# Later modulation sections summed by GpSimd during attention, inverse sums broadcast by DMA

## The chip, the core and the metric

The kernel runs on one core of one Trainium2 chip. The metric is device time in microseconds (us). The kernel before was run three times: 2298.46 us median, 2298.4 lowest, 2302.22 highest. Durations below come from one further execution under the profiler.

## The reference, cut to what matters

The reference is one layer of a block with two branches, in float32, for 1024 latent and 256 context tokens of width 1024. A conditioning vector `c` gives six modulation sections of 1024 numbers each (numbered here 0 to 5, in the order of the last line):

```python
silu_c = jax.nn.silu(c)
mod = (silu_c @ w_mod[l] + b_mod[l])[:, None, :]
sh1, sc1, g1, sh2, sc2, g2 = jnp.split(mod, 6, axis=-1)
h = rmsnorm(x, norm1_g[l]) * (1.0 + sc1) + sh1
y, yc = token_mix(h, hc, ...)
x = x + g1 * y
x = x + g2 * swiglu(rmsnorm(x, norm2_g[l]) * (1.0 + sc2) + sh2, ...)
```

`token_mix` projects `h`, runs an mLSTM scan in two directions and a grouped-query attention (8 query heads, 2 key/value heads, 1280 keys), and merges both through `w_pa`, `w_pb` and `w_o`. Sections 0 and 1 are wanted at the very start; sections 2 (`g1`), 3 (`sh2`), 4 (`sc2`) and 5 (`g2`) only behind attention.

## The kernel before

Float32 products are made of three fp32r matmuls (`mm3`, lines 104 to 106): each operand is split into a high part (ScalarE, line 98) and a low part (line 99, on GpSimd or VectorE). A planner in `run` hands out projection units one after another; a tile framework then orders every engine's queue, each queue runs in order, and semaphores do the rest. Loads and stores go through SP's queue for the most part.

The stages in time: the projections (to about 780 us) and the mLSTM heads (to about 1000 us), merging that branch with `w_pa`, attention (about 1072 to 1392 us), the `w_pb` stage (to about 1545 us), the `w_o` stage, and the feed-forward part.

**Modulation.** `mod_block` (line 285) loads 512 columns of `w_mod` in four DMAs of 512 KB and multiplies them on TensorE with `sc`, the silu of `c`, in eight float32 matmuls (line 300, tile `macc`); VectorE copies the result out (line 304). `modulation_rest` (line 333) does one half of a later section with it. For sections 2 and 5 one more matmul (line 344, tile `mg`) gives a row, VectorE adds the bias, and a DMA writes the row to `d_g`; for sections 3 and 4 four matmuls with one column (line 312, tile `mch`) turn it to channels for `B2` and `A2`. It is called eight times: after projection units 14 and 15 (line 1281, section 2), after column blocks n = 1, 2, 4 and 5 of the `w_pb` loop (line 1396, sections 3 and 4), and once in each half of the `w_o` loop (line 1508, section 5).

**Attention** (line 1083) goes through 64 steps: 2 key/value groups, 8 tiles of 128 tokens, 4 heads. A step makes scores for the next head (tile `sc`, maxima by line 1033), transposes the probabilities of this one (line 1054, tile `pt`, evacuated by lines 1057 and 1058 into `PT`), and does a part of the value products of the tile before (`attn_values`, tile `av`, `part` = the head). PSUM banks with tag Y, two of them, serve all transposes. The inverse row sums go into columns 0, 32, 64 and 96 of a 128x128 tile `dg`, which GpSimd zeroes for every tile (line 1100). In part 1 `dg` is transposed (line 1071), copied to `rrow` (line 1073), and GpSimd broadcasts four rows of it over the partitions into `rs` (line 1076). In part 3 VectorE multiplies `av` by `rs` into `yaf` (line 1080). `attn_group_kv` (line 992) splits v with the low part on GpSimd; `attn_q` (line 1012) loads the queries of a tile into the single buffer `qr`.

Of the kernel before, what the change touches and what calls it, by code (L numbers as in the profile page):

```python
# [9 lines left out]
F32 = mybir.dt.float32  # L10
F32R = mybir.dt.float32r
AF = mybir.ActivationFunctionType
ALU = mybir.AluOpType
# [4 lines left out]
P = 128  # L18
D = 1024
KT = D // P  # L20
S = 1024
CT = 256
NT = S // P
# [64 lines left out]
class Block:  # L88
# [241 lines left out]
                    nc.vector.tensor_tensor(t, v, bm[:, 8 + k:10 + k], op=ALU.add)  # L330
                    nc.vector.scalar_tensor_tensor(out=self.A1[:, s, k:k + 2], in0=t, scalar=1.0, in1=g1[:, k:k + 2], op0=ALU.add, op1=ALU.mult)

    def modulation_rest(self, ps, i):

        nc = self.nc
        bm = self.ch("b_mod")
        j0, b = (2, 5, 3, 4)[i // 2], i % 2
        c0 = j0 * D + b * 512
        rows = self.mod_block(ps, "X", (c0, c0 + 256))
        if i < 4:  # L340
            row = self.slots.get([P, 1024], F32)
            nc.sync.dma_start(row[0:1, 0:512], self.io["b_mod"][0:1, c0:c0 + 512])
            o = ps("Y", "mg")
            nc.tensor.matmul(o[0:2, :], lhsT=self.sel, rhs=rows[:, 0], start=True, stop=True)
            nc.vector.tensor_tensor(row[0:1, 512:1024], o[0:1, :], row[0:1, 0:512], op=ALU.add)
            nc.sync.dma_start(self.d_g[i // 2:i // 2 + 1, b * 512:(b + 1) * 512], row[0:1, 512:1024])
            self.slots.put(rows, row)
            return
        m = self.mod_channels(rows, ps, "Y", 1)[:, :, 0]
        hs = slice(4 * b, 4 * b + 4)  # L350
        if j0 == 3:
            nc.vector.tensor_tensor(self.B2[:, hs], m, bm[:, 24 + 4 * b:28 + 4 * b], op=ALU.add)
        else:
            t = self.st.tile([P, 4], F32, name="modt2", tag="modt2", bufs=2)
            nc.vector.tensor_tensor(t, m, bm[:, 32 + 4 * b:36 + 4 * b], op=ALU.add)
            nc.vector.scalar_tensor_tensor(out=self.A2[:, hs], in0=t, scalar=1.0, in1=self.ch("norm2_g")[:, hs], op0=ALU.add, op1=ALU.mult)


    def first_loads(self):
# [632 lines left out]
    def attn_group_kv(self, pool, ps, g):  # L992
        nc = self.nc
        kt = [pool.tile([P, NP * P], F32R, name="kT%d" % i, tag="kT%d" % i, bufs=2) for i in range(2)]
        vv = [pool.tile([P, NP, AD], F32R, name="vv%d" % i, tag="vv%d" % i, bufs=1) for i in range(2)]
        for q in range(5):
            kr = pool.tile([P, 2, AD], F32, name="kr", tag="kr", bufs=2)
            nc.sync.dma_start(kr, self.d_k[q * 256:(q + 1) * 256, g * AD:(g + 1) * AD].rearrange("(t p) d -> p t d", p=P))
            vr = pool.tile([P, 2, AD], F32, name="vr", tag="vr", bufs=2)
            nc.sync.dma_start(vr, self.d_v[q * 256:(q + 1) * 256, g * AD:(g + 1) * AD].rearrange("(t p) d -> p t d", p=P))  # L1000
            tp = ps("Y", "pt")
            for i in range(2):
                nc.tensor.transpose(tp[:, i * P:(i + 1) * P], kr[:, i], self.idf)
            sl = slice(q * 256, (q + 1) * 256)
            nc.scalar.activation(kt[0][:, sl], tp[:, 0:256], AF.Copy)
            nc.vector.tensor_tensor(kt[1][:, sl], tp[:, 0:256], kt[0][:, sl].bitcast(F32), op=ALU.subtract)
            self.split(vv[0][:, 2 * q:2 * q + 2], vv[1][:, 2 * q:2 * q + 2], vr)
        return kt, vv

    SEGS = ((0, 512), (512, 512), (1024, 256))  # L1010
# [49 lines left out]
    def attn_values(self, pool, ps, g, t, PT, vv, dg, ya, part):  # L1060

        nc = self.nc
        if part == 0:
            self.av = ps("Z", "av")
        av = self.av
        for s in ((0, 1, 2), (3, 4), (5, 6, 7), (8, 9))[part]:
            pt = PT[s // 4]
            self.mm3(av, (vv[0][:, s], vv[1][:, s]), (pt[0][:, s % 4], pt[1][:, s % 4]), s == 0, s == NP - 1)
        if part == 1:
            rb = ps("Y", "pt")  # L1070
            nc.tensor.transpose(rb[:, 0:P], dg, self.idf)
            rows = pool.tile([P, P], F32, name="rrow", tag="rrow", bufs=1)
            nc.vector.tensor_copy(rows, rb[:, 0:P])
            self.rs = pool.tile([P, 512], F32, name="rs", tag="rs", bufs=1)
            for h in range(4):
                nc.gpsimd.partition_broadcast(self.rs[:, h * P:(h + 1) * P], rows[32 * h:32 * h + 1, :])
        if part < 3:
            return
        rs = self.rs
        nc.vector.tensor_tensor(ya[:, 4 * g:4 * g + 4, t * P:(t + 1) * P], av.rearrange("p (h t) -> p h t", h=4),  # L1080
                                rs.rearrange("p (h t) -> p h t", h=4), op=ALU.mult)

    def attention(self, pool, ps):


        nc = self.nc
        kv, qs, dgs = {}, {}, {}
        kv[0] = self.attn_group_kv(pool, ps, 0)
        qs[0, 0] = self.attn_q(pool, ps, 0, 0)
        steps = [(g, t, h) for g in range(2) for t in range(NT) for h in range(4)]  # L1090

        def scores(i):
            if i >= len(steps):
                return None
            g, t, h = steps[i]
            if h == 0:
                if (g, t) not in qs:
                    qs[g, t] = self.attn_q(pool, ps, g, t)
                dgs[g, t] = pool.tile([P, P], F32, name="dg", tag="dg", bufs=2)
                nc.gpsimd.memset(dgs[g, t], 0.0)  # L1100
            sc, st = self.attn_scores(pool, ps, h, qs[g, t], kv[g][0])
            return lambda: self.attn_exp(pool, h, sc, st, dgs[g, t])

# [3 lines left out]

        yield
        pr = scores(0)()
        ptp, ya = yield  # L1110
        PT, pend = None, None
        for i, (g, t, h) in enumerate(steps):
            if g == 0 and t == NT - 2 and h == 0:
# [11 lines left out]
            if h == 3:  # L1125
                pend = (pool, ps, g, t, PT, kv[g][1], dgs[g, t], ya)
            pr = nxt() if nxt else None
        for part in range(4):
            self.attn_values(*pend, part)
        yield  # L1130
# [2 lines left out]
    def run(self):  # L1133
        nc, tc, io = self.nc, self.tc, self.io
# [8 lines left out]
        def scratch(name, shape):  # L1143
            return dr.tile(shape, F32, name=name)
# [12 lines left out]
        self.d_mm = scratch("d_mm", [D, S])  # L1157
        self.d_ms = scratch("d_ms", [D, S])
        self.d_x1 = scratch("d_x1", [S, D])
        self.d_act = scratch("d_act", [FT // 2, 7, P, 512])  # L1160

        self.const, close_const = pool("const")
# [22 lines left out]
        slots = self.slots = Slots()  # L1185
# [64 lines left out]
        X, later = {}, []  # L1250
# [5 lines left out]
        for i, u in enumerate(units):  # L1256
# [20 lines left out]
                more()  # L1277
            if i == 13:
                slots.put(*[t for p in self.cT for t in p])
            if i in (14, 15):  # L1280
                self.modulation_rest(PS, i - 14)
            if i == 22:
                while later:
                    more()
# [63 lines left out]

        pt, close_pt = pool("pt")
        w_pb = [self.load_s(slots, io["w_pb"], 0, KT, n * P, P) for n in range(2)]  # L1350
        attn.send((pt, yaf))
        close_pt()
        close_pa()

# [21 lines left out]
        for n in range(KT):  # L1376
# [15 lines left out]
                self.split(hi[:, n % 2], lo[:, n % 2], t[:, 0])  # L1392
                slots.put(t)
            slots.put(*w)
            if n in (1, 2, 4, 5):
                self.modulation_rest(PS, 3 + n if n < 3 else 2 + n)
            if n >= KT - 2:
                load_o(0, (0, 1) if n == KT - 2 else (2, 3))
        for half in range(2):
# [85 lines left out]
        for half in range(2):  # L1485
# [7 lines left out]
            for b in range(2):  # L1493
                c = slice(b * 512, (b + 1) * 512)
                for t in range(4):
# [8 lines left out]
                    if b:  # L1504
                        r0 = (4 * half + t) * P
                        nc.sync.dma_start(self.d_x1[r0:r0 + P, :], x1[t])
                if not b:
                    self.modulation_rest(PS, 2 + half)
                if half:
                    for j in range(4):  # L1510
                        slots.put(*w_o[b, j])
# [204 lines left out]
        acc = {}  # L1716
# [128 lines left out]
```

## Time and profile before

| | |
|---|---|
| median of 3 runs | 2298.46 us |
| profiled execution, whole time | 2302.7 us |
| its span, first to last instruction | 2300.6 us |
| mean granted TensorE clock | 0.979 |
| TensorE matmul busy | 2164.7 us (94%) |
| VectorE, ScalarE, GpSimd busy | 1566.8, 983.6, 755.6 us |
| DMA | 258.18 MB, mean 112 GB/s |

Whole time and span differ by 2.1 us, which lie around the first and last instruction. Times in rows count from the span's start. A matmul's duration runs longer than the distance to the next one, because matmuls are pipelined; the distance between starts is what a matmul costs.

### The profile page before, as it was taken

The page shows a single profiled execution, that of the slowest core. Times are in us where ns is not written, and L with a number is a line of the kernel's source. Part 1 is how long each engine was busy: PE and PEld are TensorE (multiplying, and loading weights), DVE is VectorE, ACT ScalarE, POOL GpSimd, SP SyncE. Part 2 cuts the span into 40 slices and gives each one's busy share as a digit, 9 for nine tenths or more (in the row PEclk, how much of TensorE's full clock was granted, in tenths as well). Part 3 has the DMA queues.
Part 4 walks back from the last instruction along what each step waited for, and adds up shares of the span by engine and source line. Part 5 has one row for each costly group of instructions (what it writes and reads, how often), then busy time and mean ns, then how long its engine had stood idle before and what let it go on. Part 6 is the DMA issues. An engine that isn't in the chain of part 4 may idle for free. (4 is left out here: it accounts for less than half of the span.)

```text
span 2300.6 us, 30283 instructions
## 1 busy us (share of the span) xinstructions
PE 2164.7 (94%) x11003; PEld 1779.5 (77%) x11003; DVE 1566.8 (68%) x2827; ACT 983.6 (43%) x1957; POOL 755.6 (33%) x615
## 2 busy tenths in 40 slices
PE   5899999999999698999999998999899999998996
PEld 2698888977978587877888886777688888876875
DVE  4767566476788777676887883345846454578997
ACT  4434435243443464543777763124523232334333
POOL 1422222321323231211101004321554544457765
PEclk9999999999999899999999999999899999999998
DMA  7122323244232813128000005652143333364421
GB/s 261 55 84 90 112 92 105 83 127 139 78 119 74 304 59 116 43 86 279 16 17 23 17 16 183 205 213 76 46 133 96 110 96 110 105 230 165 163 83 74
DMA packets 173301, 258.18 MB, mean 112 GB/s; under 512 B 13008, under 2 KB 111320, under 8 KB 173152
## 3 DMA queue, kind: packets, MB, share of 16 engines
q1 hardware_dynamic: 163232, 232.43, 30.6%
q10 hardware_dynamic: 9920, 23.82, 2.7%
q8 instruction: 87, 1.43, 0.2%
q14 instruction: 62, 0.51, 0.1%
HBM read 185.91 MB, written 70.30 MB: 111 GB/s over the span
## 5 line engine op out<-in xcount | busy, mean ns | idle before, releaser
L98 ACT ACTIVATE s<-s 128x1024 fp32r<-128x1024 f32 (+2 forms) x438 | 360.6, 846 | 661.2 <-DVE s L233 68.7
L104 PE MATMUL pr<-s,s 128*128 128x512 f32 (+1 forms) x1736 | 624.1, 361 | 19.3 <-DVE s L261 10.0
L106 PE MATMUL pr<-s,s 128*128 128x512 f32 (+1 forms) x1736 | 622.4, 359 | 7.8 <-POOL s L99 4.7
L105 PE MATMUL pr<-s,s 128*128 128x512 f32 (+1 forms) x1736 | 623.0, 359 | 5.8 <-POOL s L99 4.1
L99 POOL TENSOR_TENSOR s<-s,s 128x1024 fp32r<-128x1024 f32 (+1 forms) x195 | 397.3, 2048 | 659.8 <-ACT s L98 517.9
L99 DVE TENSOR_TENSOR s<-s,s 128x1024 fp32r<-128x1024 f32 (+2 forms) x243 | 303.8, 1258 | 131.7 <-ACT s L98 108.3
L104 PEld LDWEIGHTS pr<-s,s 128*128 128x128 f32 x1736 | 331.6, 191 | 75.6 <-ACT s L98 12.5
L106 PEld LDWEIGHTS pr<-s,s 128*128 128x128 f32 x1736 | 331.0, 191 | 60.4 <-POOL s L99 6.8
L105 PEld LDWEIGHTS pr<-s,s 128*128 128x128 f32 x1736 | 331.4, 191 | 56.7 <-POOL s L99 5.3
L104 PE MATMUL pj<-s,s 128*128 128x512 f32 x568 | 227.9, 402 | 19.3 <-DVE s L1743 14.5
L105 PE MATMUL pj<-s,s 128*128 128x512 f32 x568 | 225.6, 397 | 7.3 <-POOL s L99 7.3
L106 PE MATMUL pj<-s,s 128*128 128x512 f32 x568 | 224.7, 396 | 0.7 <-POOL s L99 0.7
L261 DVE TENSOR_TENSOR s<-s,pr 128x512 f32<-128x512 f32 x200 | 133.3, 681 | 87.8 <-PE pr L106 83.2
L1533 DVE TENSOR_TENSOR s<-s,pr 128x512 f32<-128x512 f32 x154 | 100.0, 679 | 112.3 <-ACT s L1549 63.1
L104 PEld LDWEIGHTS pj<-s,s 128*128 128x128 f32 x568 | 108.7, 191 | 54.7 <-DVE s L1743 18.5
L1058 DVE TENSOR_TENSOR PT<-pt,PT 128x512 fp32r<-128x512 f32 (+1 forms) x192 | 112.5, 598 | 33.2 <-ACT PT L1057 31.1
L1043 ACT ACTIVATE pr<-sc,st 128x512 f32<-128x512 f32 (+1 forms) x192 | 118.2, 623 | 34.4 <-DVE st L1035 34.1
L105 PEld LDWEIGHTS pj<-s,s 128*128 128x128 f32 x568 | 108.8, 192 | 30.2 <-POOL s L99 7.7
L106 PEld LDWEIGHTS pj<-s,s 128*128 128x128 f32 x568 | 108.8, 192 | 24.3 <-POOL s L99 1.1
L1543 POOL TENSOR_TENSOR s<-s,s 128x512 f32<-128x512 f32 x44 | 70.0, 1593 | 165.2 <-ACT s L98 87.6
L1057 ACT ACTIVATE PT<-pt 128x512 fp32r<-128x512 f32 (+1 forms) x192 | 94.6, 525 | 54.4 <-PE pt L1054 54.1
L1033 DVE TENSOR_REDUCE st<-sc 128x1 f32<-128x512 f32 (+1 forms) x192 | 109.6, 591 | 0.8 <-PE sc L106 0.8
(313 smaller groups left out, 3503.8 us busy)
## 6 DMA issues: line engine op xcount, KB each, us to landing
s<-in_w_in_dram SPq DMA_DIRECT2D x60, 512.0 KB
d_act<-s SPq DMA_DIRECT2D x74, 256.0 KB
s<-d_act SPq DMA_DIRECT2D x37, 512.0 KB
s<-in_w_mod_dram SPq DMA_DIRECT2D x32, 512.0 KB
s<-in_w_ffn_gate_dram SPq DMA_DIRECT2D x22, 512.0 KB
s<-in_w_ffn_up_dram SPq DMA_DIRECT2D x22, 512.0 KB
s<-in_w_ffn_down_dram SPq DMA_DIRECT2D x22, 512.0 KB
s<-in_w_mod_dram SPq DMA_DIRECT2D x32, 256.0 KB
```

Of the source, the lines that this page charges most:

```text
L98: nc.scalar.activation(hi, src, AF.Copy)
L99: (lo_eng or nc.gpsimd).tensor_tensor(lo, src, hi.bitcast(F32), op=ALU.subtract)
L104: nc.tensor.matmul(out, lhsT=lhs[0], rhs=rhs[0], start=first, stop=False)
L105: nc.tensor.matmul(out, lhsT=lhs[0], rhs=rhs[1], start=False, stop=False)
L106: nc.tensor.matmul(out, lhsT=lhs[1], rhs=rhs[0], start=False, stop=last)
L261: eng.tensor_tensor(out, a, b, op=ALU.add)
L1033: nc.vector.tensor_reduce(st[:, j:j + 1], o[:, 0:n], axis=AX.X, op=ALU.max)
L1043: nc.scalar.activation(pr[:, s0:s0 + n], sc[j][:, 0:n], AF.Exp, bias=st[:, 3:4], accum_out=st[:, 4 + j:5 + j])
L1057: nc.scalar.activation(hi, src, AF.Copy)
L1058: nc.vector.tensor_tensor(lo, src, hi.bitcast(F32), op=ALU.subtract)
L1533: nc.vector.tensor_tensor(out, a, b, op=ALU.add)
L1543: nc.gpsimd.tensor_tensor(g, g, o, op=ALU.mult)
```

## The change

The later sections are no longer multiplied on TensorE. `modulation_rest` becomes a generator that runs beside attention: for each of the four sections and each of eight blocks of 128 input channels it loads 512 KB of `w_mod` into one of two buffers `wm`; GpSimd multiplies the tile by `sc`, one number per partition, and adds it to a sum `acc`, which was zeroed and given the bias in row 0. After eight blocks TensorE sums `acc` over the partitions with a tile of ones: two matmuls for sections 2 and 5, eight with one column for sections 3 and 4. Attention takes one turn of the generator in 5 of 8 steps. The two `dg` tiles are zeroed once, by VectorE; the low part of v goes to VectorE; `dg` is transposed in part 0 in place of part 1; and the inverse sums go by DMA to a scratch tensor `d_rs` and back, spread over all partitions.

```diff
@@ -330,30 +330,56 @@
-    def modulation_rest(self, ps, i):
...
+    def modulation_rest(self, pool):
+
+
+        nc, slots, ps = self.nc, self.slots, self.ps
+        sections = (2, 3, 4, 5)
+        seq = [(j0, k) for j0 in sections for k in range(KT)]
+        loaded, accs = [], {}
+
+        def load():
+            i = len(loaded)
+            if i >= len(seq):
+                return
+            j0, k = seq[i]
+            w = pool.tile([P, D], F32, name="wm", tag="wm", bufs=2)
+            nc.sync.dma_start(w, self.io["w_mod"][k * P:(k + 1) * P, j0 * D:(j0 + 1) * D])
+            loaded.append(w)
+
+        def start(j0):
+            accs[j0] = slots.get([P, D], F32)
+            nc.gpsimd.memset(accs[j0], 0.0)
+            nc.sync.dma_start(accs[j0][0:1, :], self.io["b_mod"][0:1, j0 * D:(j0 + 1) * D])
+
+        start(sections[0])
+        load()
+        for i, (j0, k) in enumerate(seq):
+            load()
+            if k == 2 and j0 != sections[-1]:
+                start(j0 + 1)
+            acc = accs[j0]
+            nc.gpsimd.tensor_scalar(loaded[i], loaded[i], self.sc[:, k, 0:1], None, op0=ALU.mult)
+            nc.gpsimd.tensor_tensor(acc, acc, loaded[i], op=ALU.add)
+            yield
+            if k + 1 < KT:
+                continue
+            if j0 in (2, 5):
+                for b in range(2):
+                    o = ps("Y", "mg")
+                    nc.tensor.matmul(o[0:2, :], lhsT=self.ones[:, 0:2], rhs=acc[:, b * 512:(b + 1) * 512], start=True, stop=True)
+                    nc.vector.tensor_copy(acc[0:1, b * 512:(b + 1) * 512], o[0:1, :])
+                nc.sync.dma_start(self.d_g[j0 // 5:j0 // 5 + 1, :], acc[0:1, :])
+            else:
+                m = ps("Y", "mch")
+                for j in range(KT):
+                    nc.tensor.matmul(m[:, j:j + 1], lhsT=acc[:, j * P:(j + 1) * P], rhs=self.ones[:, 0:1], start=True, stop=True)
+                if j0 == 3:
+                    nc.vector.tensor_copy(self.B2, m[:, 0:KT])
+                else:
+                    nc.vector.scalar_tensor_tensor(out=self.A2, in0=m[:, 0:KT], scalar=1.0, in1=self.ch("norm2_g")[:, 0:KT], op0=ALU.add, op1=ALU.mult)
+            slots.put(accs.pop(j0))
+            yield
 
 
     def first_loads(self):
@@ -1004,7 +1030,7 @@
             sl = slice(q * 256, (q + 1) * 256)
             nc.scalar.activation(kt[0][:, sl], tp[:, 0:256], AF.Copy)
             nc.vector.tensor_tensor(kt[1][:, sl], tp[:, 0:256], kt[0][:, sl].bitcast(F32), op=ALU.subtract)
-            self.split(vv[0][:, 2 * q:2 * q + 2], vv[1][:, 2 * q:2 * q + 2], vr)
+            self.split(vv[0][:, 2 * q:2 * q + 2], vv[1][:, 2 * q:2 * q + 2], vr, nc.vector)
         return kt, vv
 
     SEGS = ((0, 512), (512, 512), (1024, 256))
@@ -1066,14 +1092,15 @@
         for s in ((0, 1, 2), (3, 4), (5, 6, 7), (8, 9))[part]:
             pt = PT[s // 4]
             self.mm3(av, (vv[0][:, s], vv[1][:, s]), (pt[0][:, s % 4], pt[1][:, s % 4]), s == 0, s == NP - 1)
-        if part == 1:
+        if part == 0:
             rb = ps("Y", "pt")
             nc.tensor.transpose(rb[:, 0:P], dg, self.idf)
-            rows = pool.tile([P, P], F32, name="rrow", tag="rrow", bufs=1)
+            rows = pool.tile([P, P], F32, name="rrow", tag="rrow", bufs=2)
             nc.vector.tensor_copy(rows, rb[:, 0:P])
             self.rs = pool.tile([P, 512], F32, name="rs", tag="rs", bufs=1)
-            for h in range(4):
-                nc.gpsimd.partition_broadcast(self.rs[:, h * P:(h + 1) * P], rows[32 * h:32 * h + 1, :])
+            i = g * NT + t
+            nc.sync.dma_start(self.d_rs[i], rows[0:P:32, :])
+            nc.sync.dma_start(self.rs, self.d_rs[i:i + 1].rearrange("o h t -> o (h t)").partition_broadcast(P))
         if part < 3:
             return
         rs = self.rs
@@ -1085,6 +1112,10 @@
 
         nc = self.nc
         kv, qs, dgs = {}, {}, {}
+
+        dg = [pool.tile([P, P], F32, name="dg%d" % i, tag="dg%d" % i, bufs=1) for i in range(2)]
+        for x in dg:
+            nc.vector.memset(x, 0.0)
         kv[0] = self.attn_group_kv(pool, ps, 0)
         qs[0, 0] = self.attn_q(pool, ps, 0, 0)
         steps = [(g, t, h) for g in range(2) for t in range(NT) for h in range(4)]
@@ -1096,8 +1127,7 @@
             if h == 0:
                 if (g, t) not in qs:
                     qs[g, t] = self.attn_q(pool, ps, g, t)
-                dgs[g, t] = pool.tile([P, P], F32, name="dg", tag="dg", bufs=2)
-                nc.gpsimd.memset(dgs[g, t], 0.0)
+                dgs[g, t] = dg[(g * NT + t) % 2]
             sc, st = self.attn_scores(pool, ps, h, qs[g, t], kv[g][0])
             return lambda: self.attn_exp(pool, h, sc, st, dgs[g, t])
 
@@ -1107,7 +1137,7 @@
 
         yield
         pr = scores(0)()
-        ptp, ya = yield
+        ptp, ya, side = yield
         PT, pend = None, None
         for i, (g, t, h) in enumerate(steps):
             if g == 0 and t == NT - 2 and h == 0:
@@ -1125,6 +1155,8 @@
             if h == 3:
                 pend = (pool, ps, g, t, PT, kv[g][1], dgs[g, t], ya)
             pr = nxt() if nxt else None
+            if i > 1 and i * 5 % 8 < 5:
+                next(side, None)
         for part in range(4):
             self.attn_values(*pend, part)
         yield
@@ -1157,6 +1189,7 @@
         self.d_mm = scratch("d_mm", [D, S])
         self.d_ms = scratch("d_ms", [D, S])
         self.d_x1 = scratch("d_x1", [S, D])
+        self.d_rs = scratch("d_rs", [2 * NT, 4, P])
         self.d_act = scratch("d_act", [FT // 2, 7, P, 512])
 
         self.const, close_const = pool("const")
@@ -1277,8 +1310,6 @@
                 more()
             if i == 13:
                 slots.put(*[t for p in self.cT for t in p])
-            if i in (14, 15):
-                self.modulation_rest(PS, i - 14)
             if i == 22:
                 while later:
                     more()
@@ -1348,7 +1379,9 @@
 
         pt, close_pt = pool("pt")
         w_pb = [self.load_s(slots, io["w_pb"], 0, KT, n * P, P) for n in range(2)]
-        attn.send((pt, yaf))
+        wm, close_wm = pool("wm")
+        attn.send((pt, yaf, self.modulation_rest(wm)))
+        close_wm()
         close_pt()
         close_pa()
 
@@ -1392,8 +1425,6 @@
                 self.split(hi[:, n % 2], lo[:, n % 2], t[:, 0])
                 slots.put(t)
             slots.put(*w)
-            if n in (1, 2, 4, 5):
-                self.modulation_rest(PS, 3 + n if n < 3 else 2 + n)
             if n >= KT - 2:
                 load_o(0, (0, 1) if n == KT - 2 else (2, 3))
         for half in range(2):
@@ -1504,8 +1535,6 @@
                     if b:
                         r0 = (4 * half + t) * P
                         nc.sync.dma_start(self.d_x1[r0:r0 + P, :], x1[t])
-                if not b:
-                    self.modulation_rest(PS, 2 + half)
                 if half:
                     for j in range(4):
                         slots.put(*w_o[b, j])
```

## Rows read from the trace of the kernel before

**Rows 1.** The page: busy time of each engine, its share of the span, instructions.
```profile
PE 2164.7 (94%) x11003; PEld 1779.5 (77%) x11003; DVE 1566.8 (68%) x2827; ACT 983.6 (43%) x1957; POOL 755.6 (33%) x615
```
**Rows 2.** Busy time by stretch (attention, then w_pb): length, PE, PEld, DVE, ACT, POOL, clock, DMA.
```profile
1072.00:1392.00 320.00, 316.55 (x1821) 261.57 (x1820) 254.29 (x638) 226.17 (x615) 31.58 (x85) 1.00 0.12 38
1392.00:1576.00 184.00, 173.79 (x802) 133.48 (x800) 69.12 (x91) 40.86 (x66) 56.46 (x31) 0.97 0.56 192
```
**Rows 3.** One tile, macc: instructions, ns min/median/max, first and last start.
```profile
L300 PE MATMUL macc<-s,sc x192: 592/593/1062, 13.2 to 1573.5; 128*32 128x512 f32 x192
```
**Rows 4.** Timeline of PE around n = 1 of w_pb: start, us, instruction.
```profile
1421.15 0.39 PE L105 MATMUL pj<-s,s 128*128 128x512 f32 x1
1421.38 0.39 PE L106 MATMUL pj<-s,s 128*128 128x512 f32 x1
1421.69 1.92 PE L300 MATMUL macc<-s,sc 128*32 128x512 f32 x16
...
1424.60 0.98 PE L312 MATMUL mch<-sel,s 128*128 128x1 f32 x8
...
1425.76 0.40 PE L106 MATMUL pj<-s,s 128*128 128x512 f32 x1
```
**Rows 5.** Timeline of PE around n = 5 of w_pb.
```profile
1474.02 0.39 PE L106 MATMUL pj<-s,s 128*128 128x512 f32 x1
...
1480.48 1.05 PE L312 MATMUL mch<-sel,s 128*128 128x1 f32 x8 [2.61 <-DVE s L304]
...
1486.04 0.39 PE L105 MATMUL pj<-s,s 128*128 128x512 f32 x1
```
**Rows 6.** Busy time by stretch, columns as in rows 2.
```profile
1480.00:1490.00 10.00, 9.52 (x39) 7.83 (x40) 5.28 (x8) 1.18 (x2) 2.14 (x1) 0.83 0.45 161
```
**Rows 7.** Timeline of PE around the modulation call after unit 14.
```profile
511.66 0.39 PE L105 MATMUL pr<-s,s 128*128 128x512 f32 x1
515.57 1.19 PE L300 MATMUL macc<-s,sc 128*32 128x512 f32 x8 [3.52 <-DMA s<-in_w_mod_dram]
...
524.73 0.40 PE L104 MATMUL pr<-s,s 128*128 128x512 f32 x1
```
**Rows 8.** Timeline of PE, the calls in the two halves of w_o.
```profile
1528.38 1.02 PE L344 MATMUL mg<-s,sel 128*2 128x512 f32 x2
...
1576.87 1.02 PE L344 MATMUL mg<-s,sel 128*2 128x512 f32 x2 [1.18 <-DVE s L304]
```
**Rows 9.** GpSimd: timeline in attention; groups by shape; line 1637's instructions.
```profile
1084.92 2.35 POOL L99 TENSOR_TENSOR s<-s,s 128x1024 fp32r<-128x1024 f32 x1 [33.69 <-ACT s L98]
...
L783 POOL MEMSET C<- 128x516 f32 x8 | 4.1, 528 | 10.4 <-PE pr L106 5.6 <-PE num L807 4.8
...
L1637 POOL TENSOR_TENSOR s<-s,s x8: 2382/3382/3416, 2043.4 to 2187.5; 128x1024 f32<-128x1024 f32 x8
```
**Rows 10.** Timelines of DVE and POOL where both work at once.
```profile
504.23 1.27 DVE L551 SCALAR_TENSOR_TENSOR s<-s,cw,s 128x1022 f32<-128x1022 f32 x1
...
505.70 2.40 POOL L99 TENSOR_TENSOR s<-s,s 128x1024 fp32r<-128x1024 f32 x1 [8.47 <-ACT s L98]
...
506.02 3.15 DVE L551 SCALAR_TENSOR_TENSOR s<-s,cw,s 128x1022 f32<-128x1022 f32 x1
...
1085.36 0.69 DVE L1058 TENSOR_TENSOR PT<-pt,PT 128x512 fp32r<-128x512 f32 x1 [1.11 <-ACT PT L1057]
```
**Rows 11.** Waits in attention: who for whom, us in total, times, longest.
```profile
PEld pt L1054 <- DVE PT L1058: 9.0, 30, 1.5
...
DVE yaf L1080 <- PE av L106: 4.6, 8, 3.3
```
**Rows 12.** Waits of SP's queue in attention, columns as in rows 11.
```profile
SPq L1016 <- DMA qr<-d_q: 27.1, 11, 2.8
```
**Rows 13.** Timelines of DVE and PE at the end of attention.
```profile
1391.99 0.69 DVE L1080 TENSOR_TENSOR yaf<-av,rs 128x512 f32<-128x512 f32 x1 [3.27 <-PE av L106]
...
1399.87 0.79 PE L105 MATMUL pj<-s,s 128*128 128x512 f32 x1 [7.29 <-POOL s L99]
```

More of the change, by code (lines that the diff above doesn't have):

```diff
@@ L331, in modulation_first @@
                     nc.vector.scalar_tensor_tensor(out=self.A1[:, s, k:k + 2], in0=t, scalar=1.0, in1=g1[:, k:k + 2], op0=ALU.add, op1=ALU.mult)
-    def modulation_rest(self, ps, i):
[L335 to L356, printed above, removed]
```

## The prediction, made before the changed kernel ran

> **What bounds the kernel now.** The page comes first: TensorE is busy 94% of the span, no other engine over 68% [rows 1]. What is taken off TensorE can therefore show in the time, unless another wait follows at once. Next come the stretches the change touches. In attention TensorE is busy 316.55 of 320 us at full clock, VectorE 254, ScalarE 226, GpSimd 32, and DMA stands at 12%; in the w_pb stage TensorE is still busy 174 of 184 us, with DMA at 56% [rows 2]. So attention has room on GpSimd and DMA and hardly any on TensorE. The tile view shows where the old modulation runs: 192 records of line 300, two for each of 96 matmuls [rows 3]; 32 matmuls belong to the first sections, which stay, and 64 (eight calls of eight) go. What a call costs has to be read in the timeline, as time by which the regular matmuls are pushed apart, because durations overlap.
>
> **What is removed.** Regular matmuls start 0.227 us apart (1421.15 to 1421.38). At n = 1 six of them start from 1421.38 up to 1425.76: 4.38 - 6 x 0.227 = 3.0 us is the call [rows 4]. Three calls repeat this (n = 1, 2, 4): 9.0 us. At n = 5 the little matmuls wait 2.61 us for VectorE's copy; from 1474.02 to 1486.04 there are 20 regular starts: 12.02 - 4.5 = 7.5 us [rows 5]. A part of that is the clock: behind the idle time the granted clock of this stretch is 0.83, so TensorE ran for some microseconds at the lower level of 1.2 GHz instead of 2.4 [rows 6]. After unit 14 TensorE waits 3.52 us for a w_mod load, and also slows down behind it; 14 regular starts lie from 511.66 to 524.73: 13.07 - 3.18 = 9.9 us [rows 7]. The call after unit 15 has the same work in two pieces and no wait, 4.6 us by the same count. In the w_o stage the first half costs 3.2 us by the same count and the second, with a wait of 1.18 us in front of its row matmul, 4.4 us [rows 8]. All eight: 9.9 + 4.6 + 9.0 + 7.5 + 3.2 + 4.4 = 38.6 us. For the call after unit 14 I take 7.5 us, between the price of its sister (4.6) and 9.9: the next unit's operands may not have been ready the whole 3.52 us either. That leaves 36.2 us. The w_mod loads, four to a call, leave these stages too; I give that no further credit, since apart from the waits already counted TensorE is full there.
>
> **What is put into attention on TensorE.** Four row matmuls at 1.02 us [rows 8], 4.1 us, and sixteen column matmuls, four times the 0.98 us of four [rows 4], 3.9 us: 8.0 us, all on the path because TensorE is full. Six new uses of the two Y banks can hold up a transpose. The nearest row is the wait of transposes for VectorE's evacuation, 9.0 us in 30 cases or 0.3 us each [rows 11]; an upper end is the bank's whole occupation, about 1.7 us (1.02 of matmul and 0.68 of VectorE). Taken: 0.3 x 6 = 2 us, ends 0 and 10.
>
> **GpSimd.** Each of 32 jobs is a multiplication and an addition of 128x1024. The addition has a row: 2.35 us in attention, 3.4 where VectorE interferes [rows 9]. The multiplication has none. Below it lies the zeroing of 128x516 in 0.528 us, so 1.05 for 1024 columns; above, the two-input addition at 3.4 [rows 9]. A pair then costs 3.4 to 6.8 us, and I take 4.0. Turns come from step 2 to step 58; a step is 320 / 64 = 5.0 us, so 32 jobs have 280 us, 8.75 us each. GpSimd keeps up over the whole range and the matmuls behind each section find their sum ready: 0 us. That cover is gone from 8.75 us a pair. The Trainium skill, page "GPSIMD Engine Reference", section "Engine selection", holds one-input work on GpSimd for roughly line rate; by its pace the multiplication would be about 1.1 us, an estimate, and the sum would not change.
>
> **VectorE against GpSimd.** Line 551, with two SBUF inputs, takes 1.27 us alone and 3.15 when an addition of GpSimd, 2.40 us long, is under way; line 1058, which reads PSUM and SBUF, takes its usual 0.69 us while GpSimd adds [rows 10]. Nearly all of VectorE's work in attention is of the second kind. The moved low parts of v are of the first: five for the second group, and two early splits of `yaf` besides. GpSimd's addition fills about 2.4 of 8.75 us, so most of them meet none; with 0.4 us each of own time and a like wait, 7 x 0.6 is 4 us on VectorE, which idles a fifth of attention; I put 2 on the path, ends 0 and 17 (seven whole additions).
>
> **Inverse sums.** The four GpSimd broadcasts go, but VectorE's line 1080 waited only for TensorE [rows 11], so they hid and nothing is won; the same holds for zeroing `dg`. The DMA way has two trips. SP's nearest row: it waited 27.1 us in 11 cases, up to 2.8, for a query load to land [rows 12]; two trips are some 5 to 6 us. Inside attention, from part 0 to part 3, 15 us hide them. Queued behind a waiting trip on SP are the query loads, issued a whole tile ahead, and the w_mod loads with 8.75 us a turn: 0 us. A w_mod load in its turn waits for the addition two jobs back, and bias rows for GpSimd's memset, at most about a pair. At the last tile no steps lie between: the transpose comes six matmuls (1.4 us) earlier, the trips add 5 to 6 in place of 1.3 of broadcasts, and line 1080, at 1391.99, may start late. TensorE then already waits 7.29 us for what follows it [rows 13]. Taken: 0.5 us, ends 0 and 3.
>
> **Sum.** 36.2 - 8.0 - 2 - 2 - 0.5 = 24 us (23.7). The profiled execution took 2302.7 us (span 2300.6 and 2.1 around it), 4.2 above the median, so the sum gives 2279 against it and 2298.5 - 24 = 2274 for the median. With no toll at all it is 38.6 - 8.0 = 30.6 us, 2268.
>
> **Rivals.**
> 1. GpSimd becomes the bound (slower). Place: the matmuls that close a section, in TensorE's queue, with everything of attention behind them. If the multiplication by a number per partition costs 8 us instead of 1 to 3.4, a pair is 10.5 us and the last section comes 32 x 1.75 = 56 us late: 2330. It decides from 8.75 us; at 9.65 the whole gain is gone. Against: no GpSimd row of this size is over 3.4 us. For: this operation has no row at all. Chance 0.10.
> 2. The DMA way is too long (no change). If SP, held by a w_mod load or a bias row that waits for GpSimd, brings `rs` more than 15 us after the transpose, VectorE stops at line 1080, and transposes stop behind it. 1.5 us in each of 16 tiles give 24 us back: 2298. For: one in-order queue now serves three waits. Against: the chain worked out above is 6 us plus at most two pairs, under 15. Chance 0.13.
> 3. GpSimd and VectorE block each other at full price: seven VectorE operations each wait for a whole addition, 7 x 2.4 = 17 us, 15 more than taken: 2289. The Trainium skill, page "GPSIMD Engine Reference", section "Key points", speaks against this change so far: GpSimd shares its SBUF interfaces with VectorE, and contends with operations that have two SBUF inputs. Line 551 agrees, 3.15 us for 1.27 [rows 10]. Against: the rest of attention's VectorE work has one PSUM input and showed no delay. Chance 0.08.
> 4. The calls go, but their time doesn't come back: TensorE, relieved, waits for the next split or load instead, and half of the 36 us stays: 18 - 12 = 6 us gained, 2292. Against: TensorE is busy in 174 of 184 us of the w_pb stage while GpSimd, VectorE and ScalarE are at 31, 38 and 22% [rows 2]. Chance 0.07.
>
> The forecast itself, 2262 to 2290, has 0.62. The range 2262 to 2298 adds rivals 3 and 4 and the better half of 2; left out are rival 1, the worse half of 2 and a little on the low side, where the reordered queues win a few microseconds more than counted. A measurement of this kernel can tell about 0.2% from no change, 4.6 us. Faster: nearly all of the forecast, most of 3 and half of 4, 0.73. Within it: half of 2, parts of 3 and 4, 0.12. Slower: rival 1 and the bad end of 2, 0.15.
>
> **What would show it.** In the changed profile: line 300 has 64 records, not 192; regular matmuls run through at n = 1, 2, 4 and 5 and after units 14 and 15; the stretch from 1392 on is some 20 us shorter, attention 10 to 13 us longer. GpSimd's pairs at 3.4 to 6.8 us, no TensorE wait for GpSimd at the closing matmuls, and no wait of line 1080 for a DMA but at the last tile would bear out the hidden parts. Wrong it is if pairs exceed 8.75 us, or if VectorE or SP stops attention in every tile.

## The result and the profile after

The changed kernel took 2333.57 us in the median of 4 runs (2330.1 to 2337.06), the kernel before on the same chip 2299.57 (2298.4 to 2302.22): a ratio of 1.0146 [1.0128, 1.0164], 34 us slower. The prediction was 24 us faster. What was to go has gone: line 300 has 64 records for 192 [rows 3]. But TensorE, busy as long as before, idles 32 us more, and GpSimd is busy 140 us longer. The engine line of the page:

```profile
PE 2164.1 (93%) x10875; PEld 1782.2 (76%) x10875; DVE 1583.1 (68%) x2827; ACT 983.5 (42%) x1955; POOL 895.8 (38%) x593
```

**Where the time went.** Three marks cut both executions into stages: the first score matmul (tile `sc`), the last `yaf` of attention, and the first transpose of the second normalization (tile `htp`). They stand in the tile view, one tile at a time: instructions, ns min/median/max, first and last start. Of the kernel before (the last `yaf` is in [rows 13]):

```profile
L104 PE MATMUL sc<-kT,qt x192: 274/392/500, 1068.2 to 1379.1; 128*128 128x512 f32 x128, 128*128 128x256 f32 x64
...
L1427 PE MATMUL htp<-idf,s x64: 270/273/475, 1577.8 to 1620.3; 128*128 128x128 f32 x64
```

Of the changed kernel:

```profile
L104 PE MATMUL sc<-kT,qt x192: 274/391/776, 1047.0 to 1421.0; 128*128 128x512 f32 x128, 128*128 128x256 f32 x64
...
L1107 DVE TENSOR_TENSOR yaf<-av,rs x16: 677/692/693, 1100.2 to 1434.2; 128x512 f32<-128x512 f32 x16
...
L1458 PE MATMUL htp<-idf,s x64: 271/273/329, 1599.4 to 1644.7; 128*128 128x128 f32 x64
```

| stage, us | before | after | difference | with the loads on GpSimd's queue (e4) |
|---|---|---|---|---|
| to the first score | 1068.2 | 1047.0 | -21.2 | 1042.5 |
| attention | 323.8 | 387.2 | +63.4 | 336.6 |
| w_pb and w_o | 185.8 | 165.2 | -20.6 | 164.6 |
| from the first `htp` on | 722.8 | 732.2 | +9.4 | 732.2 |
| span | 2300.6 | 2331.6 | +31.0 | 2275.9 |

The profiled execution of the kernel before took 2302.7 us, 3.1 above the median, so differences of single stages are uncertain by some microseconds. The calls gave back what was counted on and a little more, 41.8 us. Attention took 63 where 12.5 were allowed, and the feed-forward stage, which the diff doesn't touch, took 9 more. Of the four executions of e9 below one took 12024.51 us, in the slower state, and is left out of its time and ratio.

**Attention in the changed kernel.** Busy time by stretch (columns as in [rows 2]), first the whole, then four stretches of 20 us:

```profile
1047.00:1434.00 387.00, 343.27 (x1880) 279.18 (x1879) 267.94 (x653) 228.91 (x615) 178.90 (x73) 0.94 0.26 83
...
1110.00:1130.00 20.00, 13.38 (x78) 11.02 (x76) 8.96 (x21) 9.60 (x26) 19.75 (x8) 0.94 0.35 100
1130.00:1150.00 20.00, 11.63 (x60) 9.77 (x61) 10.27 (x27) 6.81 (x19) 19.66 (x9) 0.72 0.39 117
...
1170.00:1190.00 20.00, 19.96 (x118) 16.44 (x116) 15.84 (x40) 13.76 (x38) 13.12 (x6) 1.00 0.27 93
...
1350.00:1370.00 20.00, 19.96 (x117) 16.59 (x117) 16.76 (x42) 14.20 (x41) 0.00 (x0) 1.00 0.09 27
```

Where TensorE is full, its 118 matmuls in 20 us are as many as after the last GpSimd job (117). From 1110 to 1150 it has 138 in 40 us, GpSimd is busy throughout, and from 1130 to 1150, behind idle time of TensorE, the mean granted clock is 0.72 of 2.4 GHz. GpSimd being full is not yet a reason. The waits of attention (who for whom, us in total, times, longest) name one:

```profile
DVE yaf L1107 <- DMA rs<-d_rs: 37.3, 6, 16.0
PE pt L1080 <- DVE PT L1084: 27.8, 5, 15.0
```

VectorE waits for the inverse sums, and TensorE's transposes then for VectorE. None of the closing matmuls (`mg`, `mch`) waits for a sum. SP's own waits in attention, and its timeline over one tile (start, us, instruction):

```profile
SPq L347 <- POOL s L363: 129.4, 29, 7.7
...
SPq L1103 <- DMA d_rs<-rrow: 14.3, 12, 2.3
```

```profile
1096.14 0.38 SPq L1103 DMA_DIRECT2D rs<-d_rs  x1
1100.95 5.60 SPq L347 DMA_DIRECT2D wm<-in_w_mod_dram  x2
1106.64 0.38 SPq L1042 DMA_DIRECT2D qr<-d_q  x1
1111.53 16.20 SPq L347 DMA_DIRECT2D wm<-in_w_mod_dram  x4
1127.82 0.51 SPq L1102 DMA_DIRECT2D d_rs<-rrow  x1
1132.64 0.33 SPq L347 DMA_DIRECT2D wm<-in_w_mod_dram  x1
1133.06 0.38 SPq L1103 DMA_DIRECT2D rs<-d_rs  x1
```

Seven `w_mod` loads (line 347) stand between one `rs` (line 1103) and the next. There are two buffers `wm`, so each load waits for the addition two jobs back, one pair of 5.3 us after the other. Four of them stand before the write of this tile's sums to `d_rs` (line 1102) and one more between the write and the read. So the read is issued at 1133.06, 36.9 us after the one of the tile before. VectorE had come to line 1107 long before that, and stood still from 1121 to 1137:

```profile
1120.46 0.68 DVE L1084 TENSOR_TENSOR PT<-pt,PT 128x512 fp32r<-128x512 f32 x1
1137.16 0.69 DVE L1107 TENSOR_TENSOR yaf<-av,rs 128x512 f32<-128x512 f32 x1 [16.02 <-DMA rs<-d_rs]
```

```profile
1138.33 1.09 PE L1080 MATMUL pt<-idf,pr 128*128 128x128 f32 x4 [14.95 <-DVE PT L1084]
```

The jobs (tile `wm`) were meant to be even over steps 2 to 58. They are not:

```profile
L347 SPq DMA_DIRECT2D wm<-in_w_mod_dram x32: 327/328/1347, 1058.0 to 1281.9; - x32
...
L362 POOL TENSOR_SCALAR wm<-wm,sc x32: 2837/2847/3267, 1066.0 to 1287.1; 128x1024 f32<-128x1024 f32 x32
L363 POOL TENSOR_TENSOR s<-s,wm x32: 2339/2394/2413, 1071.6 to 1290.0; 128x1024 f32<-128x1024 f32 x32
```

The last starts at 1290, 144 us before attention ends. A pair is 2.85 + 2.39 = 5.24 us, and GpSimd did most of them back to back, from 1066 to 1161, 1182 to 1221 and 1254 to 1292. What comes between is the zeroing of a new sum, which waits 9.6 us for the closing of one section and 29.8 us for that of another:

```profile
POOL s L352 <- PE mch L376: 29.8, 1, 29.8
POOL s L352 <- DMA d_g<-s: 9.6, 1, 9.6
```

Nothing in the program ties a single job to a step: the turns of the generator only set where its instructions stand in the order in which the program is written.

### The profile page after: what moved, and what is told of

It is laid out like the page before. It is cut to its first block, busy times and chain, and to the rows that moved or that the text cites. A ratio compares the mean times of both kernels' runs of the same rounds, so it can differ in the third digit from the quotient of the medians.

```text
span 2331.6 us, 30006 instructions
## 1 busy us (share of the span) xinstructions
PE 2164.1 (93%) x10875; PEld 1782.2 (76%) x10875; DVE 1583.1 (68%) x2827; ACT 983.5 (42%) x1955; POOL 895.8 (38%) x593
## 5 line engine op out<-in xcount | busy, mean ns | idle before, releaser
L99 DVE TENSOR_TENSOR s<-s,s 128x1024 fp32r<-128x1024 f32 (+2 forms) x243 | 310.5, 1286 | 131.3 <-ACT s L98 101.2
L1080 PE MATMUL pt<-idf,pr 128*128 128x128 f32 x640 | 100.6, 282 | 28.1 <-DVE PT L1084 27.8
```

The lines of the kernel that those rows point to most:

```text
L99: (lo_eng or nc.gpsimd).tensor_tensor(lo, src, hi.bitcast(F32), op=ALU.subtract)
L1080: nc.tensor.transpose(tp[:, i * P:(i + 1) * P], pr[:, s0 + i * P:s0 + (i + 1) * P], self.idf)
```

## The experiments

**Theory Q**: the loads wait on SP for GpSimd, and the DMAs of the inverse sums, and of the queries, wait behind them in the same queue. **Rivals**: GpSimd's work disturbs VectorE through the memory that both use; the DMA way of the sums is too long by itself; 16 MB of `w_mod` crowd the other transfers. For the feed-forward stage a second question came up on the way. All ratios are to runs of the kernel before on the same chip, each with its 95% interval.

**e3_rs_alone: the DMA way alone.** The kernel before with the hunks on `rs`, `dg` and the low part of v; modulation stays as it was.

```diff
-            for h in range(4):
-                nc.gpsimd.partition_broadcast(...)
+            nc.sync.dma_start(self.d_rs[i], rows[0:P:32, :])
+            nc.sync.dma_start(self.rs, self.d_rs[i:i + 1]...partition_broadcast(P))
```

> The kernel before with everything of the change but the modulation: inverse sums by DMA from part 0 on, tiles zeroed once, low parts of v on VectorE. Theory Q: SP's queue holds nothing that waits for GpSimd, so the DMA way hides but at the last tile: 2297 to 2304, attention 323 to 328 us. Theory D (the DMA way itself is too slow): 2315 or more.

Measured: 2296.8 us, 0.9987 [0.9975, 1.0]; attention 324.1 for 323.8. The two trips cost nothing while nothing stands in front of them. VectorE waits for `rs` once, 5.5 us at the last tile.

**e1_no_loads: GpSimd's work without the loads.** GpSimd multiplies and adds two tiles that stay in place; the sections are therefore not those of the reference.

```diff
-            w = pool.tile([P, D], F32, name="wm", tag="wm", bufs=2)
-            nc.sync.dma_start(w, self.io["w_mod"][...])
+            if i < 2:
+                w = pool.tile([P, D], F32, name="wm%d" % i, tag="wm%d" % i, bufs=1)
+                nc.sync.dma_start(w, self.io["w_mod"][...])
+            else:
+                w = loaded[i % 2]
```

> The later w_mod loads are left out but for the first two: GpSimd does all 32 multiplications and additions on two resident tiles, so sections 2 to 5 hold other numbers. Theory Q (the loads stand in SP's in-order queue waiting for GpSimd's buffers, and hold up the inverse sums and queries queued behind them): no wait of line 1107's kind for rs beyond 2 us, attention back to 325 to 340 us from 387, time 2265 to 2285. Theory P (VectorE and GpSimd block each other on SBUF): GpSimd's work is all there, so attention stays at 375 us or more, time 2320 or more. Theory D (the DMA way of the inverse sums is too slow by itself): 2310 or more, with waits for rs.

Measured: 2281.19 us, 0.9927 [0.9912, 0.9942]; attention 338.3. All of GpSimd's work is there, and 49 of the 63 us are gone. That leaves little for the first rival: attention is 14.5 us above the kernel before, near the 12.5 that the prediction allowed.

**e2_no_late_mod: nothing put into attention.** Sections 2 to 5 are left out; their biases stand in for them.

```diff
-        attn.send((pt, yaf, self.modulation_rest(wm)))
...
+        attn.send((pt, yaf, iter(())))
```

> Sections 2 to 5 are left out (the biases stand in for them): no loads, no GpSimd jobs, no closing matmuls; the DMA way of the inverse sums, the tiles zeroed once and the low parts of v on VectorE stay. It prices what the removed calls are worth. All theories but D: attention 320 to 328 us, and 21 us less both before attention and behind it than in the kernel before: 2255 to 2265. Theory D: attention 380 us, time 2310 or more.

Measured: 2268.55 us, 0.9875 [0.986, 0.989], above what was expected. Attention is 328.7, and from the first `htp` on it takes 733.1 us, as in the changed kernel, though no later section is computed at all. The 9 us of the feed-forward stage thus belong neither to GpSimd nor to the loads.

**e4_gp_queue: the same work, loads issued by GpSimd.** In its own queue a load waits behind the addition that it needs anyway. Nothing is left out.

```diff
-            nc.sync.dma_start(w, self.io["w_mod"][...])
+            nc.gpsimd.dma_start(w, self.io["w_mod"][...])
...
-            nc.sync.dma_start(accs[j0][0:1, :], self.io["b_mod"][...])
+            nc.gpsimd.dma_start(accs[j0][0:1, :], self.io["b_mod"][...])
```

> The w_mod loads and bias rows are issued from GpSimd's queue, everything else as in the changed kernel. Theory Q: SP's queue has only queries and inverse sums, line 1107 waits under 2 us, attention 330 to 345 us, time 2268 to 2290. Theory P: attention stays at 375 us or more, time 2320 or more, and a little more for issuing on GpSimd.

Measured: 2279.53 us (2276.94 to 2283.6), 0.9921 [0.9903, 0.994]. Its attention by stretch, its wait for `rs` (one, at the last tile, where the expectation had under 2 us), and its additions:

```profile
1042.00:1379.00 337.00, 331.51 (x1881) 270.29 (x1881) 270.22 (x655) 227.20 (x615) 192.16 (x105) 0.99 0.29 94
```

```profile
DVE yaf L1107 <- DMA rs<-d_rs: 4.8, 1, 4.8
```

```profile
L363 POOL TENSOR_TENSOR s<-s,wm x32: 2359/2396/2426, 1065.8 to 1270.1; 128x1024 f32<-128x1024 f32 x32
```

This settles the main cause. The same 16 MB in the same stage, the same GpSimd work and even the same crowding of the jobs (all within 1066 to 1270) cost 50.6 us less once SP doesn't wait for GpSimd. Set the two rows of attention side by side: 1880 and 1881 matmuls; TensorE's idle time 43.7 us and 5.5; its busy time 343.3 and 331.5. Of the 50 us, 38 are waits, and 12 are matmuls that run longer, in an attention with a mean granted clock of 0.94 for 0.99. The loads of e4 also run through another DMA queue; e5 and e10 below, in which they stay on SP and 43 and 44 of the 51 us go all the same, leave little of the loss to that.

**e9_rs_act: the other way round.** The loads stay on SP; ScalarE issues the two DMAs of the sums.

```diff
-            nc.sync.dma_start(self.d_rs[i], rows[0:P:32, :])
-            nc.sync.dma_start(self.rs, ...)
+            nc.scalar.dma_start(self.d_rs[i], rows[0:P:32, :])
+            nc.scalar.dma_start(self.rs, ...)
```

> The changed kernel with the two DMAs of the inverse sums issued from ScalarE's queue; w_mod loads, bias rows and query loads stay on SP. If the inverse sums are what the loads held up (theory Q as the waits show it): 2280 to 2300. If the queries held up behind the loads stop attention as much: attention stays over 365 us, 2310 or more. If ScalarE loses as much by waiting on its own queue for VectorE's row and the first trip, 2300 to 2320, with waits of line 1069 or 1083 in their place.

Measured: 2326.05 us (2324.14 to 2327.84), 1.011 [1.0086, 1.0135]; attention 378.3: the second of the three cases expected, in which the queries behind the loads stop attention as much. The `rs` waits are nearly gone (one of 6.5 us), but the same queue holds the queries. SP's timeline, and TensorE's:

```profile
1110.63 32.04 SPq L347 DMA_DIRECT2D wm<-in_w_mod_dram  x7
1142.77 0.38 SPq L1042 DMA_DIRECT2D qr<-d_q  x1
```

```profile
1146.98 1.09 PE L1045 MATMUL pt<-idf,qr 128*128 128x128 f32 x4 [5.85 <-DMA qr<-d_q]
```

And ScalarE now stands still itself: the read of the sums waits in its queue, and the evacuations wait behind the read:

```profile
1100.72 0.51 ACTq L1102 DMA_DIRECT2D d_rs<-rrow  x1
...
1103.27 0.22 ACT L1069 ACTIVATION_READ_ACCUMULATOR pr<-sc,st 128x1 f32 x1
1109.29 0.32 ACTq L1103 DMA_DIRECT2D rs<-d_rs  x1
1109.65 0.87 ACT L1083 ACTIVATE PT<-pt 128x256 fp32r<-128x256 f32 x2 [6.17 <-DMA wm<-in_w_mod_dram]
```

TensorE idles 38.4 of 379 us in this attention; the waits put 12.9 of them down directly to the queries and keys behind the loads, and how the rest divides between the two queues wasn't separated. One victim was taken out of the queue, and the next came forward. What has to leave the queue is the waiting load, not what waits behind it.

**e5_tied: jobs tied to steps, loads on SP.** The multiplier is a little tile `tie` that VectorE writes from the running step's `st` times 0 plus `sc`, so that a job can't start before its step.

```diff
-            nc.gpsimd.tensor_scalar(loaded[i], loaded[i], self.sc[:, k, 0:1], None, op0=ALU.mult)
+            tie = pool.tile([P, 1], F32, name="tie", tag="tie", bufs=2)
+            nc.vector.scalar_tensor_tensor(out=tie, in0=self.now[:, 7:8], scalar=0.0, in1=self.sc[:, k, 0:1], op0=ALU.mult, op1=ALU.add)
+            nc.gpsimd.tensor_scalar(loaded[i], loaded[i], tie, None, op0=ALU.mult)
...
```

> Each multiplication takes its number from a little tile that VectorE writes from the running step's statistics, so a job cannot start before its step of attention; the loads stay on SP. Theory Q: GpSimd's jobs and the loads now stand at 2 to 3 a tile, SP waits little, attention 332 to 350 us, time 2270 to 2295. Theory P: the same overlap of GpSimd and VectorE, spread thinner, attention 370 us or more, time 2315 or more. Theory R (pairs of 5.3 us are too slow whatever their order): TensorE waits for GpSimd at closing matmuls, over 2300.

Measured: 2287.37 us, 0.9960 [0.9948, 0.9973]; attention 344.4. Its multiplications, and SP's wait for GpSimd:

```profile
L364 POOL TENSOR_SCALAR wm<-wm,tie x32: 2843/2848/2854, 1069.7 to 1345.6; 128x1024 f32<-128x1024 f32 x32
```

```profile
SPq L347 <- POOL s L365: 167.2, 30, 11.2
```

The jobs now do lie over the whole of attention, and 43 of the 51 us come back, although SP waits longer in total (167 for 129 us). It isn't the sum of SP's waits that counts, but how long the loads between one read of the sums and the next hold the queue: seven loads in the tile shown above, two or three in each tile here while the jobs last.

**e10_add_only: shorter jobs, loads on SP.** The multiplication is left out (the sums lack the factor `sc`).

```diff
-            nc.gpsimd.tensor_scalar(loaded[i], loaded[i], self.sc[:, k, 0:1], None, op0=ALU.mult)
```

> The changed kernel without GpSimd's multiplication (it is left out, so sections 2 to 5 hold plain column sums): a job is the addition alone, 2.4 us in place of 5.24; loads, bias rows, inverse sums and queries stay on SP as they are. Theory Q: a load at SP's head then waits 2.4 us or less, the up to seven loads in front of an inverse sum cost 17 us in place of 37 and fit into a tile's 19; attention 332 to 348 us from 387, time 2272 to 2292. If it is the order of SP's queue alone, whatever GpSimd's pace: attention over 370 us, 2315 or more.

Measured: 2284.48 us (2280.94 to 2289.98), 0.9944 [0.9925, 0.9963]; attention 343.2.

```profile
SPq L347 <- POOL s L362: 61.4, 28, 3.7
```

With jobs of 2.4 us for 5.2 SP waits half as long, and 44 of the 51 us are gone, although as many as eight loads still stand between two reads of the sums, issued 26.9 us apart. The loss grows faster than the job, which fits with only that showing which passes the 15 us between part 0 and part 3.

**The feed-forward stage.** Its matmuls are the same instructions. By stretch, 40 us of line 104 to 106's product for tile `pr`, in the kernel before and in the changed one:

```profile
1697.80:1737.80 40.00, 40.00 (x178) 33.12 (x177) 22.61 (x32) 13.16 (x19) 18.25 (x12) 1.00 0.31 99
```

```profile
1722.50:1762.50 40.00, 40.00 (x175) 32.50 (x174) 22.84 (x32) 12.80 (x18) 18.70 (x12) 1.00 0.31 99
```

TensorE is busy all the time, at full granted clock in both, but 178 matmuls pass in one and 175 in the other: one starts every 0.2267 or every 0.231 us. Over the 1848 of this tile in the stage that is some 8 of the 9.4 us of the table. The change dropped the little tiles `modt2`, two of 16 bytes a partition, allocated ahead of the large tiles, so by the order of allocation all later tiles lie at other addresses (the traces hold none); and the old calls took and gave back slots, so the free list stands in another order. Two kernels were set against each other, both e4 with one addition:

**e6_pad: two tiles `modt2` allocated again** ahead of the slots, and used for nothing.

```diff
+        for i in range(2):
+            nc.vector.memset(self.st.tile([P, 4], F32, name="modt2", tag="modt2", bufs=2), 0.0)
```

> The kernel with loads from GpSimd's queue, and the two little tiles modt2, which the change drops, allocated again, so that every later tile lies at the address it had before. Theory A (addresses): feed-forward matmuls come every 0.2267 us again in place of 0.231, 2270 to 2274. Theory S (which slots hold the operands): no change, 2277 to 2283.

**e7_rotate: the free list turned** by as many slots as the old calls turned it, at the same eight places.

```diff
+        def turn_slots(n):
+            for j in range(n):
+                slots.free.append(slots.free.pop(0))
...
```

> The kernel with loads from GpSimd's queue, and the list of free slots turned at the eight places where the removed calls took and gave back slots, as far as they turned it. Theory S: the feed-forward operands lie in the slots of before, matmuls come every 0.2267 us again, 2268 to 2275. Theory A: no change, 2277 to 2283.

Measured: e6 2274.52 us (2272.25 to 2280.09), 0.9890 [0.9871, 0.991], half a microsecond above theory A's range, and 724.3 us from the first `htp` on, for 732.2 in e4; the matmuls are back at their pace:

```profile
1668.60:1708.60 40.00, 40.00 (x178) 33.14 (x177) 22.64 (x33) 13.10 (x19) 18.22 (x12) 1.00 0.31 99
```

e7 took 2288.16 us, 0.9947 [0.9931, 0.9963], with 732.9 us there and a matmul every 0.230; and its stages ahead of attention are 15 us longer than e4's, which neither theory had foreseen and whose cause wasn't tried. So the pad, which moves the addresses of all later tiles and otherwise adds two small memsets, gives the pace back; the turned list doesn't. All 13 kernels divide the same way: in the five with the two tiles (the kernel before, e3, e6, e11, e12) the stage takes 722.8 to 726.1 us, in the eight without them 732.1 to 734.6.

**e12_after_pad: the pad alone** (the changed kernel, loads on SP, with the lines of e6).

> The changed kernel with the two little tiles modt2 allocated again, nothing else. Theory A (addresses): feed-forward matmuls every 0.2267 us, the stretch from the first norm transposes to the end 723 to 725 us in place of 732, time 2322 to 2329. Otherwise 2331 to 2336.

Measured: 2324.14 us (2320.8 to 2329.92), 1.0116 [1.0089, 1.0143]. From the first `htp` on 726.1 us for 732.2 (723 to 725 expected), and 178 matmuls in 40 us; attention is 385.1 as before the pad. The two losses are separate: 51 us of queue, 6 to 8 of addresses.

**e11_tied_gp_pad: everything together** (e6 with the tie of e5).

> All repairs together: loads from GpSimd's queue, jobs tied to their steps, the two little tiles back. Theory Q: with loads off SP it no longer matters whether the jobs are spread, so the same as without the tie, 2270 to 2279. If bunched jobs still cost something by overlapping VectorE: 2262 to 2270.

Measured: 2281.38 us, 0.9926 [0.9904, 0.9948], just above what was expected. Attention is 346.2 for 336.1 in e6: once SP is free of the loads, spreading the jobs wins nothing. Why it costs 10 us wasn't tried. **e6 is the best version**: it computes all that the reference asks for, and is 1.1% faster than the kernel before.

## Why the prediction was wrong, step by step

**The step that failed** stands under "Inverse sums": "Queued behind a waiting trip on SP are the query loads, issued a whole tile ahead, and the w_mod loads with 8.75 us a turn: 0 us. A w_mod load in its turn waits for the addition two jobs back, … at most about a pair." It was right that a load waits about a pair. It was wrong that one load at a time waits. The 8.75 us a turn came from the sentence "Turns come from step 2 to step 58; a step is 320 / 64 = 5.0 us, so 32 jobs have 280 us", which took the order in which the program is written for a schedule in time. Up to seven loads stood in one tile, and three of them at 5.3 us already use up the 15 us that hide the trips.

**The rival** with this place was the second, at 0.13: "SP, held by a w_mod load or a bias row that waits for GpSimd, brings `rs` more than 15 us after the transpose". Place and mechanism were right. Its price, 1.5 us in each of 16 tiles, was not: the loss was 51 us, in five tiles or so of up to 16 us wait each, with the slower matmuls behind each. "6 us plus at most two pairs, under 15" should have been two trips plus as many pairs as the queue can hold there. Even two pairs were not safe: with the prediction's own 3.4 to 6.8 us a pair they come to 12.8 to 19.6 us, with the measured 5.24 to 16.5.

**The steps that held:**
- Removed calls: 36.2 us taken, 38.6 counted; the two stages are 41.8 us shorter. Rival 4, that their time would not come back, falls.
- Toll of attention: 12.5 taken; with the queue mended (e4) it is 12.8. That these agree is in part luck. In e2, which has no later section at all, attention is already 4.9 us longer than before. The first 40 us show it, in the kernel before, in e2 and in e4:

```profile
1068.20:1108.20 40.00, 37.15 (x199) 29.71 (x198) 31.38 (x72) 22.13 (x58) 4.94 (x3) 1.00 0.48 162
1041.50:1081.50 40.00, 35.20 (x177) 28.17 (x176) 29.00 (x66) 20.69 (x54) 4.75 (x2) 0.96 0.48 163
1042.50:1082.50 40.00, 37.32 (x193) 30.13 (x192) 30.85 (x71) 21.44 (x56) 19.89 (x14) 0.96 0.58 198
```

e2 is 22 matmuls behind, some 5 us at 0.2267 each; why it starts more slowly wasn't tried. e4 is 16 ahead of e2 there, some 3.6 us. So the 7.9 us by which attention grows from e2 to e4 stand for some 11.5 (an estimate from these rows): the closing matmuls, 8.0 by the prediction's rows, and about 3.5 for the rest of GpSimd's work, of which 2.5 are found below.

- GpSimd: the multiplication took 2.85 us within the bounds 1.05 to 3.4, the pair 5.24 where 4.0 was taken within 3.4 to 6.8. Rival 1 falls: a pair is far from 8.75, and no closing matmul waited.
- VectorE against GpSimd: 2 us taken, rival 3 at 15 more. In e4 it happened once on the path. One of the two low parts of v in the row shown took 2.92 us where the others take 0.42, beside an addition of GpSimd, and TensorE then waited 2.47 us:

```profile
L99 DVE TENSOR_TENSOR vv<-vr,vv x10: 415/418/2919, 1017.0 to 1238.7; 128x256 fp32r<-128x256 f32 x10
...
1232.80 3.45 DVE L99 TENSOR_TENSOR vv<-vr,vv 128x256 fp32r<-128x256 f32 x2
1233.59 2.38 POOL L363 TENSOR_TENSOR s<-s,wm 128x1024 f32<-128x1024 f32 x1
1237.25 0.38 PE L104 MATMUL sc<-kT,qt 128*128 128x256 f32 x1 [2.47 <-ACT pr L1069]
```

In e2, where GpSimd adds nothing, none of the ten takes over 0.43 us. So the 2 us were right in place and in size, and rival 3's price of seven whole additions falls. The Trainium skill, page "GPSIMD Engine Reference", section "Key points", names contention for VectorE operations with two SBUF inputs; these rows and those of before [rows 10] agree, and attention holds few such operations.

- The DMA way itself: 0.5 us, ends 0 and 3; e3 puts it at 0.3 in attention, and the wait at the last tile came as described (4.8 us in e4, where 3.27 of waiting for TensorE stood before [rows 13]).

**Two sums of the working** don't come out, and the result didn't turn on them: the gain of 24 us is used up at 8.75 + 24 / 32 = 9.5 us a pair, not at 9.65; and "0.4 us each of own time and a like wait" is 0.8 and not 0.6, so 5.6 us for seven.

**What no step had** is the feed-forward stage. The prediction ended at the `w_o` stage, because the diff did. With the queue and these 9 us put right, e6 takes 2274.5 us, next to the 2274 of the sum. That it comes so close is partly luck: in the traces of e6 and the kernel before, the stages around attention are 43.9 us shorter where 36.2 were taken, and the spans differ by 30.1 us, the medians by 25.2.

## What to carry to other kernels

A load that waits for a free buffer holds everything behind it in its queue, so a transfer with a deadline must not share an in-order queue with a load whose buffer is freed by a slower engine; let the engine that frees the buffer issue the load. Handing out turns of a generator evenly spreads nothing in time: unless a dependence ties a job to a step, it runs as soon as its inputs are there, and how long such loads hold the queue in the worst tile, not in the mean, is what has to be hidden. After a change, look at the pace of matmuls in stages that the diff doesn't touch.

## What the runs showed of the hardware

- GpSimd's multiplication of 128x1024 by one number per partition took 2.85 us, longer than the two-input addition of the same shape, 2.39. The Trainium skill, page "GPSIMD Engine Reference", section "Engine selection", holds one-input work for roughly line rate, some 1.1 us here by the prediction's estimate; the trace differs, and the measurement decides.
- A shift of later tiles by 32 bytes a partition (by the order of allocation; the traces hold no addresses) changed the spacing of equal matmuls from 0.2267 to 0.231 us at full granted clock, and a pad of that size changed it back in three kernels (e6, e11, e12; 178 matmuls in 40 us for 175). Why an address does this isn't shown.
- In e9 a DMA on ScalarE's queue that waits for another DMA's landing kept ScalarE idle for 6.17 us in the stretch shown; the profile puts that down to a `w_mod` load that landed last. Whether the write of the sums was slow behind that load wasn't tried.
